# One address distance per stage, and 512-column matmuls in one up projection, in a two-layer hybrid decoder

## The chip, the cores and the metric

The kernel runs on one core of one Trainium2 chip. The metric is device time in microseconds (us) for one execution of the whole program; two runs of the kernel before gave 2269.54 and 2273.31 us, a median of 2271.43 us.

## The reference, cut to what matters

`x` has one sequence of 256 positions and 2048 channels, in float32. It goes through two layers and a last RMS norm. One layer is

```python
x = x + mixed(rms_norm(x) @ w_in) @ w_out            # w_in 2048 x 6400, w_out 2048 x 2048
h = rms_norm(x) @ w_up                               # 2048 x 11264
acc = conv_b + sum(conv_w[j] * shift(h, 2 - j) for j in range(3))
gate, val = split(acc, 2)
x = x + (silu(gate) * val) @ w_down                  # 5632 x 2048
```

`mixed` is three token mixers side by side (retention, dilated attention, a gated MLP over positions). They cost little here: the weights are 3168 blocks of 128 x 128 a layer, and nearly all of the time goes into multiplying each of them once with the 256 positions.

## The kernel before, in words

All activations are held transposed, channels on the 128 partitions and the 256 positions along the free axis (`S = 256`, `P = 128`). The program computes in float32 with TensorE's `float32r` type: every operand is split into a rounded high part and a low part, and a product is the sum of three matmuls, high times high, high times low and low times high.

**Weights.** They stream from HBM in 792 pieces of 128 x 1024 numbers, in the order of use (class `Weights`). ScalarE copies a piece to `hi` (line 113), VectorE subtracts to get `lo` (line 123). `hi` and `lo` have four buffers each, and a piece is split three pieces before its use. One piece is eight blocks of 128 x 128. `take` hands out the next block; at the first block of a piece it also calls `step`, and each call moves the evacuations that are under way on by one `yield`. So the order of instructions on ScalarE and VectorE is written out by this count and not by a scheduler.

**Projections with the activations moving** (`proj_t`, matmul at line 355). For a block of the weights the weights are loaded into the array, and 256 columns of the activation operand stream through. An operand tile holds its high part in the first 256 columns and its low part in the next 256. In layer 0 a block's three matmuls are `hi` with the high part, `hi` with the low part, `lo` with the high part; in layer 1 the order is `hi`, `lo`, `hi`. An output tile `m` takes 16 blocks (12 in the last part of the down projection), its sum stands in the first 256 of the 512 columns of a PSUM bank, and there are four such banks (`mm`). Operands are `p` tiles (the normalised input, for `w_in` and `w_up`) or `q` tiles (mixer outputs, for `w_out`; gated values, for `w_down`).

**Projections with the weights moving** (`proj_n`, matmul at line 395), for those parts of `w_in` whose result is wanted with positions on the partitions. Here the `p` tile is loaded and 256 columns of `hi` or `lo` stream.

**The FFN** runs in three parts of 16, 16 and 12 gated tiles (`FFN_PARTS`): up projection of a part, then its share of the down projection. `up_evac` takes an up projection's sum: `scaled` (line 366) multiplies it by the norm's factor `rbc` into `hs`, then come the convolution, the gate, and the split into a `q` tile (lines 736 and 738).

**The q tiles.** Sixteen slots in one pool; `q_tile` allots 2 * 256 + 112 float32 numbers, 2496 bytes in each partition, and returns 512 of them from a start that depends on `which`. There are eight values of `which`: `w_out`, and the three parts of `w_down`, in each of two layers.

Of the kernel before, what the change touches and what calls it, by code (L numbers as in the profile page):

```python
# [21 lines left out]
F32 = mybir.dt.float32  # L22
F32R = mybir.dt.float32r
AF = mybir.ActivationFunctionType
ALU = mybir.AluOpType
AX = mybir.AxisListType

P = 128
D = 2048
S = 256  # L30
# [123 lines left out]
def trunk_kernel(tc, x0, xt, stream, par, cst, wst, lnw, out):  # L154
# [3 lines left out]
    V, A, T, GP = nc.vector, nc.scalar, nc.tensor, nc.gpsimd  # L158
    ctx = ExitStack()
    with ctx:  # L160
        E = ctx.enter_context

        def pool(name, bufs=1):
            return E(tc.tile_pool(name=name, bufs=bufs))

        cp, xp, pp, qp = pool("cst"), pool("xres"), pool("px"), pool("qx")
# [25 lines left out]
        def until(cond):  # L192
            n = 0
            while not cond():
                n += 1
                assert n < 100
                step(0)
                step(1)

        def run(g):  # L200
            ev.append(g)

        W = Weights(nc, stream, raw, hp, lp, 3, step)
        live = [0]

        def mm():
            until(lambda: live[0] < 4)
            live[0] += 1
            return ps.tile([P, 512], F32, name="mm", tag="mm")

        def mt():
            return mm()[:, 0:S]
# [22 lines left out]
        make_identity(nc, ident)  # L235
        ones = cp.tile([P, P], F32, name="ones")
        GP.memset(ones, 1.0)
        mhalf = cp.tile([P, 12], F32, name="mhalf")
        GP.memset(mhalf, -0.5)
        hs_bufs = [cp.tile([P, S + 2], F32, name=f"hs{i}") for i in range(4)]  # L240
        for t in hs_bufs:
# [7 lines left out]
        norm = {"n": 0}  # L249
# [88 lines left out]
        def proj_t(mat, l, rows, cols, opnd, evac, lead):  # L338


            n = len(rows)
            groups = [list(range(lead))] + [[m] for m in range(lead, len(cols))]
            for g in groups:
                fast[0] = lead > 0 and W.pos > 0 and (len(g) > 1 or g[0] == len(cols) - 1)
                acc = {m: mt() for m in g}
                sz = 8 if len(g) > 1 else n
                for k0 in range(0, n, sz):
                    for m in g:
                        for k in range(k0, min(k0 + sz, n)):
                            x = opnd(k)  # L350
                            hi, lo = W.take(mat, l, rows[k], cols[m], P)
                            xh, xl = x[:, 0:S], x[:, S : 2 * S]
                            terms = ((hi, xh), (hi, xl), (lo, xh)) if l == 0 else ((hi, xh), (lo, xh), (hi, xl))
                            for i, (w, v) in enumerate(terms):
                                T.matmul(acc[m], w, v, start=k == 0 and i == 0, stop=k == n - 1 and i == 2)  # L355
                        if k == n - 1:
                            run(evac(m, acc[m]))

        def moved(acc):

            t = temp()
            A.activation(t, acc, AF.Copy)
            live[0] -= 1
            return t

        def scaled(acc, out):

            if norm["ready"]:
                V.tensor_tensor(out, acc, norm["bc"], op=ALU.mult)  # L369
                live[0] -= 1  # L370
            else:
                t = moved(acc)
                yield
                yield from normed()
                V.tensor_tensor(out, t, norm["bc"], op=ALU.mult)

        def normed():
            while not norm["ready"]:
                yield

        def temp():
            return fw.tile([P, S], F32, name="t", tag="t", bufs=4)
# [24 lines left out]
            return QX[k]  # L407


        STARTS = [b // 4 for b in (0, 128, 320, 384, 448, 64, 192, 256)]  # L410

        def q_tile(slot, which):
            a = STARTS[which]
            return qp.tile([P, 2 * S + 112], F32R, name=f"q{slot}", tag=f"q{slot}")[:, a : a + 2 * S]

        def mixed_block(slot, l, src, c0):

            t = mx()
            for j in range(2):
                T.transpose(t[:, j * P : (j + 1) * P], src[j][:, c0 : c0 + P], ident)  # L420
            q = q_tile(slot, 4 * l)
            w = prm[:, C_MIX + l * NK + slot : C_MIX + l * NK + slot + 1]
            yield
            split_hi(q, t[:, 0:S], w)
            split_lo(q, t[:, 0:S], w)
            QX[slot] = q
# [189 lines left out]
        for l in range(DEPTH):  # L616
# [8 lines left out]
            def att_qk(m, acc):  # L625
                h, half = m // 2, m % 2
                if half == 0:
                    aqk[h] = qp.tile([P, 2 * S], F32, name=f"aqk{h}", tag=f"q{Q_ATT + h}")
                yield from scaled(acc, aqk[h][:, half * S : (half + 1) * S])

            proj_t("w_in", l, allrows, [c + h * P for h in range(H) for c in (AQ, AK)], p_of, att_qk, 4)
            fast[0] = False

# [18 lines left out]
            def ret_qk(m, acc):  # L652
# [12 lines left out]
                V.tensor_tensor(o, o, sw, op=ALU.add)  # L665

            proj_t("w_in", l, allrows, [c + h * P for h in range(H) for c in (RQ, RK)], p_of, ret_qk, 0)

            rv = pair("rv", 768)
# [28 lines left out]

            PX[:] = [None] * NK
            proj_t("w_out", l, MIX_ROWS, [m * P for m in range(NK)], q_of, ev_out(C_N2 + l * NK), 4)  # L700

            norm["ready"] = False
# [9 lines left out]
            def up_evac(f0, part):  # L712
                gate = {}

                def ev_up(m, acc):
                    f, val = f0 + m // 2, m % 2
                    ch = f + NF * val
                    hs = hs_bufs[hsn[0] % len(hs_bufs)]
                    hsn[0] += 1
                    yield from scaled(acc, hs[:, 2 : S + 2])  # L720
                    yield
                    a = wk.tile([P, 512], F32, name="a", tag=A_TAGS[an[0] % 4])[:, 0:S]
                    an[0] += 1
                    A.activation(a, hs[:, 2 : S + 2], AF.Identity, scale=conv_col(ch, 2), bias=conv_col(ch, 3))  # L724
                    yield
                    V.scalar_tensor_tensor(a, hs[:, 1 : S + 1], conv_col(ch, 1), a, op0=ALU.mult, op1=ALU.add)  # L726
                    V.scalar_tensor_tensor(a, hs[:, 0:S], conv_col(ch, 0), a, op0=ALU.mult, op1=ALU.add)  # L727
                    yield
                    if val == 0:
                        A.activation(a, a, AF.Silu)  # L730
                        gate[f] = a
                        return
                    V.tensor_tensor(a, a, gate.pop(f), op=ALU.mult)  # L733
                    yield
                    q = q_tile(f - f0, part)
                    A.activation(q[:, 0:S], a, AF.Copy)  # L736
                    yield
                    V.tensor_tensor(q[:, S : 2 * S], a, q[:, 0:S].bitcast(F32), op=ALU.subtract)
                    QX[f - f0] = q
                return ev_up  # L740
# [15 lines left out]
        bc = norm["bc"][:, None, :].to_broadcast([P, 2, S])  # L756
# [93 lines left out]
```

## Time and profile before

| what | value |
| --- | --- |
| median of two runs | 2271.43 us |
| time of the profiled execution | 2269.97 us |
| its span, first to last instruction | 2268.2 us |
| TensorE busy, share of the span | 99% |
| matmuls | 19430 |
| VectorE busy, ScalarE busy | 64%, 50% |
| HBM read | 420.06 MB, 186 GB/s |
| granted TensorE clock, share of full speed | 0.998 |

A busy span of a matmul covers its whole way through the array, and the spans of successive matmuls overlap (a 256-column matmul is booked with 277 ns and the next begins some 113 to 120 ns later). So the busy share says that TensorE never waits long, but not how fast it works; the pace is read from the time that a counted run of matmuls took. The stages, by time in the trace: layer 0's `w_in` to 310 us, `w_out` to 402, then up and down projections by parts to 578 and 669, 843 and 934, 1065 and 1133 us. Layer 1: `w_in` to 1433, `w_out` to 1525, up and down to 1700 and 1791, 1965 and 2056, 2187 and 2255 us.

### The profile page before, as it was taken

To read this page: it belongs to the slowest core of one execution; us is meant where nothing else is said; L and a number is where in the kernel's file an instruction comes from. 1 tells how busy PE (TensorE), PEld (TensorE's weight loads), DVE (VectorE), ACT (ScalarE), POOL (GpSimd) and SP (SyncE) were. 2 spreads that over 40 slices of the span, in tenths; PEclk is the share of its full clock that TensorE was granted. 3 is DMA by queue.
4 is the path that set the end of the run, shared out by engine and by line. 5 is a ranking of instruction groups with operands and counts; after the bars stand their busy time and mean duration, and the time that the engine had idled before them with its cause. 6 is when DMAs were issued, how large, how long until landed. Compare 5 with 4: busy or idle time off the path is not lost.

```text
span 2268.2 us, 45995 instructions
## 1 busy us (share of the span) xinstructions
PE 2251.2 (99%) x19430; PEld 2248.1 (99%) x19430; DVE 1443.3 (64%) x2086; ACT 1143.5 (50%) x1616; POOL 21.8 (1%) x39
## 2 busy tenths in 40 slices
PE   9999999999999999999999999999999999999997
PEld 8999999999999999999999999999999999999997
DVE  6565556677547775577655655667775577656765
ACT  6475554555435553455544644555554355434553
POOL 0000000000000000000000001000000000000000
PEclk9999999999999999999999999999999999999999
DMA  8545445555555555565555454555555555555553
GB/s 283 193 158 187 160 168 194 188 194 195 186 186 196 195 182 197 179 206 189 184 201 180 164 180 168 178 184 192 193 192 188 185 199 193 194 186 189 193 191 126
DMA packets 117135, 425.15 MB, mean 187 GB/s; under 512 B 12992, under 2 KB 12992, under 8 KB 116800
## 3 DMA queue, kind: packets, MB, share of 16 engines
q1 hardware_dynamic: 116928, 422.21, 54.8%
q8 instruction: 152, 2.49, 0.4%
q14 instruction: 55, 0.45, 0.1%
HBM read 420.06 MB, written 2.10 MB: 186 GB/s over the span
## 4 chain that ended last, share of the span: by engine, by line
PE 99%; DMA 0%; DVE 0%; SPq 0%; ACT 0%; POOLq 0%; issue 0%; DVEq 0%
PE mm L355 84%; PE mm L395 13%; PE mx L420 0%; DMA xg<-in_xt_dram 0%; PE mx L435 0%; PE mx L489 0%; DVE xg L760 0%; PE mx L310 0%; PE mx L450 0%; PE mx L554 0%; PE mx L458 0%; PE mx L500 0%; PE mx L459 0%; PE mx L501 0%; PE mx L499 0%; PE mx L434 0%
## 5 line engine op out<-in xcount | busy, mean ns | idle before, releaser
L123 DVE TENSOR_TENSOR lo<-raw,hi 128x1024 fp32r<-128x1024 f32 (+1 forms) x793 | 969.0, 1223 | 710.4 <-ACT hi L113 710.2
L113 ACT ACTIVATE hi<-raw 128x1024 fp32r<-128x1024 f32 (+1 forms) x793 | 837.5, 1058 | 881.8 <-PE mm L355 490.7
L355 PE MATMUL mm<-p,hi 128*128 128x256 f32 x7168 | 1235.4, 277 | 5.5 <-ACT hi L113 5.2
L355 PEld LDWEIGHTS mm<-p,hi 128*128 128x128 f32 x7168 | 1084.6, 188 | 6.9 <-ACT hi L113 5.2
L355 PE MATMUL mm<-p,lo 128*128 128x256 f32 x3584 | 991.8, 277 | 0.0
L355 PE MATMUL mm<-q,hi 128*128 128x256 f32 x3840 | 684.8, 281 | 0.0
L355 PEld LDWEIGHTS mm<-p,lo 128*128 128x128 f32 x3584 | 674.3, 188 | 0.5 <-DVE lo L123 0.2
L355 PEld LDWEIGHTS mm<-q,hi 128*128 128x128 f32 x3840 | 589.3, 188 | 0.0
L355 PE MATMUL mm<-q,lo 128*128 128x256 f32 x1920 | 538.4, 280 | 0.0
L355 PEld LDWEIGHTS mm<-q,lo 128*128 128x128 f32 x1920 | 361.6, 188 | 0.0
L395 PE MATMUL mm<-hi,p 128*128 128x256 f32 x1664 | 272.1, 279 | 0.0
L395 PEld LDWEIGHTS mm<-hi,p 128*128 128x128 f32 x1664 | 231.2, 188 | 0.0
L395 PE MATMUL mm<-lo,p 128*128 128x256 f32 x832 | 179.3, 278 | 0.0
L724 ACT ACTIVATE a<-hs,prm 128x256 f32<-128x256 f32 x176 | 104.1, 591 | 63.3 <-DVE hs L369 63.3
L395 PEld LDWEIGHTS mm<-lo,p 128*128 128x128 f32 x832 | 133.3, 188 | 0.0
L727 DVE SCALAR_TENSOR_TENSOR a<-hs,prm,a 128x256 f32<-128x256 f32 x176 | 85.3, 485 | 6.3
L726 DVE SCALAR_TENSOR_TENSOR a<-hs,prm,a 128x256 f32<-128x256 f32 x176 | 84.2, 478 | 4.4 <-ACT a L724 4.4
L692 DVE TENSOR_TENSOR xg<-xg,mm 128x256 f32<-128x256 f32 x128 | 53.3, 418 | 50.7 <-PE mm L355 50.7
L369 DVE TENSOR_TENSOR hs<-mm,rbc 128x256 f32<-128x256 f32 x176 | 73.5, 418 | 2.7 <-PE mm L355 2.7
L730 ACT ACTIVATE a<-a 128x256 f32<-128x256 f32 x88 | 35.6, 405 | 33.5 <-DVE a L727 33.5
L279 ACT ACTIVATE t<-xg 128x256 f32<-128x256 f32 x75 | 30.1, 408 | 39.9 <-DVE xg L692 38.9
L736 ACT ACTIVATE q<-a 128x256 fp32r<-128x256 f32 x88 | 35.4, 403 | 3.5 <-DVE a L733 3.5
(120 smaller groups left out, 578.4 us busy)
## 6 DMA issues: line engine op xcount, KB each, us to landing
raw<-in_stream_dram SPq DMA_DIRECT2D x791, 512.0 KB, 3.4
out_dram<-xg SPq DMA_DIRECT2D x8, 256.0 KB, 2.4
xg<-in_xt_dram SPq DMA_DIRECT2D x3, 512.0 KB, 8.6
cs<-in_cst_dram SPq DMA_DIRECT2D x1, 1216.0 KB, 8.7
raw<-in_stream_dram SPq DMA_DIRECT2D x2, 256.0 KB, 4.2
ws<-in_wst_dram SPq DMA_DIRECT2D x2, 256.0 KB, 4.5
lw<-in_lnw_dram SPq DMA_DIRECT2D x2, 256.0 KB, 4.7
prm<-in_par_dram SPq DMA_DIRECT2D x1, 412.0 KB, 6.0
```

The costliest lines, as they stand in the source:

```text
L113: self.nc.scalar.activation(hi[:, h], src[:, h], AF.Copy)
L123: self.nc.vector.tensor_tensor(lo[:, h], src[:, h], hi[:, h].bitcast(F32), op=ALU.subtract)
L279: A.activation(sq, X[j], AF.Square)
L355: T.matmul(acc[m], w, v, start=k == 0 and i == 0, stop=k == n - 1 and i == 2)
L369: V.tensor_tensor(out, acc, norm["bc"], op=ALU.mult)
L395: T.matmul(acc[j][:, c], v, w[:, c], start=k == 0 and i == 0 and c.start == 0, stop=k == NK - 1 and i == 2, skip_group_check=True)
L692: V.tensor_tensor(X[m], X[m], acc, op=ALU.add)
L724: A.activation(a, hs[:, 2 : S + 2], AF.Identity, scale=conv_col(ch, 2), bias=conv_col(ch, 3))
L726: V.scalar_tensor_tensor(a, hs[:, 1 : S + 1], conv_col(ch, 1), a, op0=ALU.mult, op1=ALU.add)
L727: V.scalar_tensor_tensor(a, hs[:, 0:S], conv_col(ch, 0), a, op0=ALU.mult, op1=ALU.add)
L730: A.activation(a, a, AF.Silu)
L736: A.activation(q[:, 0:S], a, AF.Copy)
```

## The change

It has three parts.

1. A `q` slot is 2 * 256 + 128 numbers, 2560 bytes, five times 512. All slots then start at the same address modulo 512, and so do all the operands of one `which`. `STARTS` is written as the wanted distance `r` less 192.
2. In the up projection of layer 1 (`wide`), a block's two matmuls with `hi` become one with 512 columns, high and low part of the operand side by side; its sum fills all 512 columns of the bank. The matmul with `lo` adds to the first 256. For the last block of an output tile the `lo` matmul comes first. `scaled` then copies the second half of the bank to a temporary on ScalarE, and VectorE adds the first half to it before the multiplication with `rbc`.
3. `mhalf` is 2 columns wide, where it was 12.

```diff
-        mhalf = cp.tile([P, 12], F32, name="mhalf")
+        mhalf = cp.tile([P, 2], F32, name="mhalf")
...
-                acc = {m: mt() for m in g}
+                wide = mat == "w_up" and l == 1
+                acc = {m: mm() if wide else mt() for m in g}
...
                             hi, lo = W.take(mat, l, rows[k], cols[m], P)
+                            if wide:
+                                if k == n - 1:
+                                    T.matmul(acc[m][:, 0:S], lo, x[:, 0:S], start=False, stop=False)
+                                T.matmul(acc[m], hi, x, start=k == 0, stop=k == n - 1)
+                                if k < n - 1:
+                                    T.matmul(acc[m][:, 0:S], lo, x[:, 0:S], start=False, stop=False)
+                                continue
...
         def scaled(acc, out):
 
-            if norm["ready"]:
+            if acc.shape[1] > S:
+                t = temp()
+                A.activation(t, acc[:, S : 2 * S], AF.Copy)
+                yield
+                V.tensor_tensor(t, t, acc[:, 0:S], op=ALU.add)
+                live[0] -= 1
+                yield from normed()
+                V.tensor_tensor(out, t, norm["bc"], op=ALU.mult)
+            elif norm["ready"]:
                 V.tensor_tensor(out, acc, norm["bc"], op=ALU.mult)
...
-        STARTS = [b // 4 for b in (0, 128, 320, 384, 448, 64, 192, 256)]
+        STARTS = [(r - 192) % 512 // 4 for r in (448, 128, 256, 0, 160, 64, 384, 224)]
 
         def q_tile(slot, which):
             a = STARTS[which]
-            return qp.tile([P, 2 * S + 112], F32R, name=f"q{slot}", tag=f"q{slot}")[:, a : a + 2 * S]
+            return qp.tile([P, 2 * S + 128], F32R, name=f"q{slot}", tag=f"q{slot}")[:, a : a + 2 * S]
```

The places of the tiles in the built programs, as bytes modulo 512 within a partition. "Distance" is the operand's start less the weights' start, modulo 512, which all blocks of a stage share where the last column names one value, since pieces, blocks and the two halves of an operand are multiples of 512 bytes.

| tile or stage | before | after |
| --- | --- | --- |
| `hi`, `lo` blocks | 0 | 480 |
| `p` tiles | 192 | 160 |
| distance `p` to weights (`w_in`, `w_up`) | 192 | 192 |
| `q` slots in the order of memory | 192, 128, 64, 0, 448, ... (64 less each) | 160, all |
| distance in `w_out`, layer 0 | all eight multiples of 64 | 448 |
| in `w_down`, layer 0, three parts | all eight multiples of 64 | 128; 256; 0 |
| in `w_out`, layer 1 | all eight multiples of 64 | 160 |
| in `w_down`, layer 1, three parts | all eight multiples of 64 | 64; 384; 224 |

Before, a stage's operands come in an order in which the distance mostly falls by 64 from one block to the next. In the first part of layer 0's `w_down` it is 320, 256, 192, 128, 64, 0, 64, 0 for slots 0 to 7; in the last part of layer 1's it is 448 for slot 0, then 384.

TensorE's order at the start of layer 1's up projection (`p` and `q` are operand tiles, `hi` and `lo` weights, `mm` the sums), before:

```order
L355 MATMUL mm<-q_17577,hi_18432 128x256
L355 MATMUL mm<-p_17643,hi_18466 128x256
L355 MATMUL mm<-p_17643,lo_18467 128x256
L355 MATMUL mm<-p_17643,hi_18466 128x256
L355 MATMUL mm<-p_17679,hi_18466 128x256
L355 MATMUL mm<-p_17679,lo_18467 128x256
L355 MATMUL mm<-p_17679,hi_18466 128x256
```

The same place in the changed program:

```order
L363 MATMUL mm<-q_17577,hi_18432 128x256
L356 MATMUL mm<-p_17643,hi_18466 128x512
L358 MATMUL mm<-p_17643,lo_18467 128x256
L356 MATMUL mm<-p_17679,hi_18466 128x512
L358 MATMUL mm<-p_17679,lo_18467 128x256
```

Three matmuls of 256 columns for a block became one of 512 and one of 256, with one weight load less; there are 1408 blocks in this projection, and nothing else changed its place on TensorE.

VectorE's order over the first two evacuations of the same projection (`t` is the temporary, `a` the convolution's sum, `lo` the split of a later piece), before:

```order
L123 TENSOR_TENSOR lo_18713<-raw_18580,hi_18712 128x1024
L369 TENSOR_TENSOR hs_124<-mm,rbc 128x256
L123 TENSOR_TENSOR lo_18746<-raw_18610,hi_18745 128x1024
L726 SCALAR_TENSOR_TENSOR a<-hs_124,prm,a 128x256
L727 SCALAR_TENSOR_TENSOR a<-hs_124,prm,a 128x256
L369 TENSOR_TENSOR hs_125<-mm,rbc 128x256
```

The same place in the changed program:

```order
L123 TENSOR_TENSOR lo_18681<-raw_18580,hi_18680 128x1024
L380 TENSOR_TENSOR t<-t,mm 128x256
L383 TENSOR_TENSOR hs_124<-t,rbc 128x256
L123 TENSOR_TENSOR lo_18707<-raw_18602,hi_18706 128x1024
L742 SCALAR_TENSOR_TENSOR a<-hs_124,prm,a 128x256
L743 SCALAR_TENSOR_TENSOR a<-hs_124,prm,a 128x256
L380 TENSOR_TENSOR t<-t,mm 128x256
L383 TENSOR_TENSOR hs_125<-t,rbc 128x256
```

Each evacuation has one VectorE instruction more, the addition, and stands one `step` later in the program, behind a copy `t<-mm` on ScalarE (line 378 of the changed kernel).

## Rows read from the trace of the kernel before

**Rows 1.** The page, busy time by engine.

```profile
PE 2251.2 (99%) x19430; PEld 2248.1 (99%) x19430; DVE 1443.3 (64%) x2086; ACT 1143.5 (50%) x1616; POOL 21.8 (1%) x39
```

**Rows 2.** Chain of waits, layer 1's up projection: start us, us, engine, tile, line, count.

```profile
1534.27 165.94 PE mm L355 x1464
...
1790.89 174.32 PE mm L355 x1538
...
2055.78 130.92 PE mm L355 x1155
```

**Rows 3.** Chain of waits in the eight stages on q tiles, in their order.

```profile
319.62 82.64 PE mm L355 x696
...
577.58 91.41 PE mm L355 x769
...
843.00 91.02 PE mm L355 x769
...
1064.48 67.55 PE mm L355 x568
...
1442.28 82.28 PE mm L355 x695
...
1700.10 90.91 PE mm L355 x768
...
1964.98 91.03 PE mm L355 x769
...
2186.47 68.64 PE mm L355 x578
```

**Rows 4.** Chain of waits within layer 0's input projection and mixers.

```profile
130.82 2.74 PE mm L355 x24
...
134.89 2.83 PE mm L355 x24
...
187.32 32.64 PE mm L395 x288
...
229.58 14.14 PE mm L395 x120
```

**Rows 5.** The same chain, matmuls on plain float32 operands.

```profile
120.29 0.33 PE mx L450 x3
...
134.45 0.43 PE mx L435 x2
```

**Rows 6.** Timeline of TensorE, first part of layer 0's down projection: start us, length.

```profile
580.14 0.41 PE L355 MATMUL mm<-q,hi 128*128 128x256 f32 x2
580.38 0.29 PE L355 MATMUL mm<-q,lo 128*128 128x256 f32 x1
580.51 0.40 PE L355 MATMUL mm<-q,hi 128*128 128x256 f32 x2
```

**Rows 7.** Timeline of TensorE, entry into layer 1's last down projection.

```profile
2186.42 0.28 PE L355 MATMUL mm<-p,hi 128*128 128x256 f32 x1
2186.53 0.28 PE L355 MATMUL mm<-q,hi 128*128 128x256 f32 x1
2186.65 0.28 PE L355 MATMUL mm<-q,lo 128*128 128x256 f32 x1
2186.76 0.40 PE L355 MATMUL mm<-q,hi 128*128 128x256 f32 x2
```

**Rows 8.** Busy time by engine in an up projection of layer 1, clock, DMA.

```profile
1790.90:1965.10 174.20, 174.20 (x1539) 174.20 (x1539) 125.15 (x187) 91.95 (x126) 0.00 (x0) 1.00 0.58 192
```

**Rows 9.** Groups by line: busy us, mean ns of one, idle before.

```profile
L362 ACT ACTIVATE t<-mm 128x256 f32<-128x256 f32 x28 | 10.8, 385 | 44.4 <-PE mm L355 40.8 <-PE mx L310 3.3 <-DVE sqacc L284 0.2
...
L733 DVE TENSOR_TENSOR a<-a 128x256 f32<-128x256 f32 x88 | 36.8, 418 | 0.2
```

**Rows 10.** Timeline of VectorE, last operand of layer 1's last part.

```profile
2192.21 0.42 DVE L738 TENSOR_TENSOR q<-a,q 128x256 fp32r<-128x256 f32 x1
```

## The prediction

> **What bounds the kernel now.** First the page: TensorE and its weight loads are busy for 99% of the span, VectorE for 64%, ScalarE for 50% [rows 1]. So no stage waits long for weights or evacuations, and the time is the number of matmuls times the interval between their starts. The chain of waits gives that interval, since it counts matmuls in unbroken stretches. In layer 1's up projection it is 165.94 / 1464 = 113.3 ns, and the same in the other two parts [rows 2]. In the eight stages whose moving operand is a `q` tile, it is 118.7, 118.9, 118.4, 118.9, 118.4, 118.4, 118.4 and 118.8 ns [rows 3], with the same instruction, the same 256 columns and the same weight buffers. The clock is granted in full, at its 2.4 GHz level [rows 8], where 256 columns are 106.7 ns; so 6.6 ns are lost with a `p` operand and some 12 with a `q` operand.
>
> What differs is the address. `p` operands keep one distance to the weights, `q` operands change it from block to block. But distance is not all. With one and the same distance, TensorE has two intervals: weights that stream against `p` tiles take 32.64 / 288 = 113.3 ns at 187 us and 14.14 / 120 = 117.8 ns at 230 us, after float32 matmuls of the retention came between; and runs of 24 with `p` moving take 2.74 or 2.83 us, 117.9 ns at the longer, after interruptions alike [rows 4]. I read this as a rhythm of the two read streams, weights and moving operand, that either settles (113.3) or does not (117.8), and that stays as it is until something interrupts it. A step in distance interrupts it at each block: one block's three matmuls after such a step took 0.37 us, from 580.14 to 580.51 [rows 6], or 123 ns each. But a step from 192 to 448 did not: at the entry into the last part the starts go on at 0.11, 0.12 and 0.11 us [rows 7].
>
> **The change, term by term.** The sum is made against the profiled execution, 2269.97 us, which is 1.5 us under the median of 2271.43; I give the result against the median.
>
> *The wide up projection.* Each of 1408 blocks now takes three intervals, 0.340 us [rows 2]. It will take one matmul of 512 columns and one of 256. No row has 512 columns of this type. Nearest is the plain float32 matmul of 256 columns, which takes about twice as long as a `float32r` one: two take 0.43 us, so 0.215 to 0.22 each [rows 5], with one weight load beside each. With a settled 113.3 for the short one this makes 0.330 us, with an unsettled 117.8 it makes 0.335. I take the middle, 0.3325, since the new pair has two unequal windows and neither rhythm is shown for it: 7.5 ns less, 1408 x 7.5 ns = 10.6 us. Upper bound: the short one at the pace of 128-column float32 matmuls, 0.33 / 3 = 0.110 [rows 5], together 0.325, a gain of 21 us. Lower bound: the short one at the worst 0.123 [rows 6] and the long one at 0.220, 0.343, a loss of 4 us.
>
> A rule speaks against the size of this gain. The Trainium skill, "TensorE: Matmul & The Clock Gate", Back-to-back issue gap, gives a warm matmul N / 2.4 + 2.5 ns; then a merge saves one 2.5 ns, an estimate of 1408 x 2.5 = 3.5 us. It would also put 256 columns at 109 ns, and the trace, with 113.3 and 118.4, does not agree.
>
> *The evacuation of the wide sums.* It adds 88 copies on ScalarE, 385 ns each, and 88 additions on VectorE at 418 ns [rows 9]: 34 and 37 us. They lie beside the matmuls. In the part at 1791 us VectorE is busy for 125.15 of 174.20 us and ScalarE for 91.95 [rows 8]; 32 evacuations add 13.4 and 12.3 us, and in a stage of some 170 us that is 81% and 61%. The copy waits for the sum in ScalarE's queue ahead of the split of a piece that is used three pieces, over 8 us, later. The chain to the next operand grows by one step, at most a piece of 24 matmuls or 2.7 us [rows 4]. The latest operand of the last part is finished at 2192.63 us [rows 10], and slot 11 is first read 105 matmuls after the stage's start at 2186.53 [rows 7], at 118.8 ns each 2199.0; so 6.4 us of cover become 3.7. Cost zero. If the cover were gone, each of the three parts would wait for the excess, one to three us in all. A sum's bank is held up to one piece longer; with four banks and 5.3 us an output tile, that delays nothing.
>
> *The q stages.* 5760 matmuls take 683 us at the intervals of rows 3. What one distance makes of each, no row shows except for 192 and, at the entry, 448. Bounds: the settled 113.3 for all, 653 us, a gain of 30.5 us; the worst block's 123 for all, 708 us, a loss of 25 us. I take by stage:
> - 448, `w_out` of layer 0: settled, by [rows 7]; 768 x 5.4 ns = 4.1 us.
> - 160 and 224, in layer 1: 32 bytes from 192, nearer to it than any other stage, but no operand of the kernel before has such a distance. I take half of the way to 113.3: 768 x 2.55 + 576 x 2.75 ns = 3.5 us.
> - 128, 256, 0, 64 and 384: unsettled, 117.8, since all that [rows 4] has for an interruption of unknown phase is the one or the other, and the q stages pass through these distances without settling. 768 x (1.1 + 0.6 + 0.6 + 0.6) + 576 x 1.1 ns = 2.9 us.
>
> Together 10.5 us. The row 123 is far from these, since it follows a step up in distance, and steps are what goes.
>
> The Trainium skill, "SBUF — State Buffer", Who interferes with whom, says that "PE and ACT never wait on anyone" and gives TensorE independent read ports for weights and moving operand. By that, distance changes nothing and this term is 0. The two intervals of like instructions in rows 2 and 3 speak against it, though they do not prove the address to be the cause.
>
> `STARTS`, `mhalf` and the longer slots add no instruction; DMAs keep their number, size and order. The weights' buffers start 32 bytes off their former place, for a DMA share of 0.58 [rows 8], which has cover.
>
> Sum: 10.6 + 10.5 = 21 us; 2271.4 - 21 = **2250 us** (2249 for a profiled execution like that before).
>
> **The rivals.**
> - *All eight stages settle.* For: 113.3 holds for whole up projections; nothing interrupts a stage of `w_down`. Against: the unsettled 14.14 us stretch also had one distance. 30.5 us, and 13.4 with a settled pair of 0.3305: 2227.5 us.
> - *The distance does nothing*, as the page's rule has it, or the rhythm of no stage settles: the q stages keep their time. For: both intervals occur at equal distance [rows 4]. Against: [rows 2, 3]. 2271.4 - 10.6 = 2261 us.
> - *The merged matmul pays little*: the loss is a part of each 256 columns, and the long matmul loses it twice; 2.5 ns remain a block, 3.5 us. For: [rows 5] is of another type, which takes twice the time for as many columns. Then 2271.4 - 3.5 - 10.5 = 2257 us.
> - *Slower: the shift by 32 bytes spoils the up projection.* `p` and weights keep 192 between them, but both now start 32 bytes past a multiple of 64, and no row has such operands. If reads go by longer lines, each stream touches one more. The 7680 matmuls of 256 columns that run at 113.3 now (4224 in layer 0's `w_up`, 2304 with `p` and 1152 with weights moving in `w_in`) would go to 117.8 and cost 34.6 us; with a wide pair of 0.335 (7 us) and q stages at 117.8 (4.6 us) that is 2294 us. It decides from 21 us / 7680 = 2.7 ns on, an interval of 116.0 in the up projection of layer 0. Against: the distance itself is the same.
>
> **How the numbers follow.** The forecast has 0.46, all settled 0.15, no effect of distance 0.19, little from the merge 0.12, slower 0.06, and 0.02 for what I did not think of. The likeliest is 2250 us. The range reaches down to 2228, where all settle, and up to 2266, where the distance does nothing and the merge half of its due; outside are half of the all-settled cases, the slower rival and the odd ones, not quite 0.2. The mark of 2%, about what a measurement of this kernel can tell from no change, lies at 2226 and 2317 us. Faster than that needs all settled and a pair of under 0.330: 0.06. Slower than that needs over 120 ns in the up projection of layer 0: 0.02.
>
> **What would show it.** Layer 1's up projection: blocks of 0.33 us, near 468 us of matmuls where there were 479, VectorE near 81%, no wait at its ends. `w_out` of layer 0: 113.3 ns but for the stretch with interruptions; distances 160 and 224 between 113 and 118; the other five near 117.8. Layer 0's up projection still at 113.3. The forecast is wrong if a stage with one distance goes above 119, if the pair stays at 0.34, or if matmuls of layer 0's up projection take over 114 ns.

## The result, and the profile after

The changed kernel takes 2298.05 us (median of two runs, 2297.86 and 2298.23), where the kernel before takes 2271.43 us. The ratio is 1.0117, with a 95% interval of 1.0074 to 1.0161: 26.6 us slower, outside the forecast range of 2228 to 2266 us. The granted clock is 0.998 in both. The first line of the page shows that TensorE is still the bound, now with fewer and partly longer matmuls; it answers to [rows 1].

```profile
PE 2279.6 (99%) x18022; PEld 2210.8 (96%) x18022; DVE 1474.5 (64%) x2174; ACT 1176.2 (51%) x1704; POOL 21.8 (1%) x39
```

So the time must be in the intervals between matmuls. The table takes each stage of the two traces from its first matmul to the first of the next stage, with the mean interval between starts of 256-column matmuls. "Distance" is the operand's start less the weights', modulo 512.

| stage | before, us (ns) | after, us (ns) | difference, us |
| --- | --- | --- | --- |
| `w_in`, layer 0, all | 304.92 | 307.65 | +2.7 |
| of it, first run of 576 on `p` | 71.89 (113.65) | 73.62 (116.79) | +1.7 |
| `w_out`, layer 0, distance 448 | 91.96 (118.77) | 87.92 (113.47) | -4.0 |
| up, layer 0, part 1 | 175.54 (113.42) | 182.02 (117.64) | +6.5 |
| up, layer 0, parts 2 and 3 | 304.68 (113.35) | 304.67 (113.35) | 0.0 |
| down, layer 0: 128; 256; 0 | 91.31; 90.91; 68.52 | 91.14 (118.67); 92.14 (119.98); 69.10 (119.97) | +1.6 |
| `w_in`, layer 1, all | 299.77 | 303.00 | +3.2 |
| `w_out`, layer 1, distance 160 | 91.69 (118.40) | 91.86 (118.64) | +0.2 |
| up, layer 1, the wide one | 175.53; 174.09; 130.56 | 181.96; 180.68; 135.51 | +18.0 |
| down, layer 1: 64; 384; 224 | 90.91; 90.93; 68.27 | 90.45 (117.77); 91.14 (118.67); 68.04 (118.33) | -0.5 |
| sum | | | +27.7 |

The spans differ by 28.0 us (2268.2 and 2296.2), so the table holds nearly all of it. Three things made it: the wide up projection lost 18.0 us, three stages that the change did not seem to touch lost 12.4, and the q stages gained 2.7 where 10.5 were forecast.

**The wide matmul.** TensorE's timeline of the changed kernel, first blocks of layer 1's up projection after an interruption by the norm (start us, length, operation). The length covers the way through the array; what counts is the time from start to start.

```profile
1541.45 0.39 PE L356 MATMUL mm<-p,hi 128*128 128x512 f32 x1
1541.67 0.28 PE L358 MATMUL mm<-p,lo 128*128 128x256 f32 x1
1541.79 0.39 PE L356 MATMUL mm<-p,hi 128*128 128x512 f32 x1
1542.02 0.28 PE L358 MATMUL mm<-p,lo 128*128 128x256 f32 x1
1542.14 0.39 PE L356 MATMUL mm<-p,hi 128*128 128x512 f32 x1
1542.37 0.28 PE L358 MATMUL mm<-p,lo 128*128 128x256 f32 x1
1542.48 0.40 PE L356 MATMUL mm<-p,hi 128*128 128x512 f32 x1
1542.72 0.28 PE L358 MATMUL mm<-p,lo 128*128 128x256 f32 x1
1542.84 0.40 PE L356 MATMUL mm<-p,hi 128*128 128x512 f32 x1
```

The first pair takes 0.34 us, as three settled matmuls did in [rows 2]; the fourth takes 0.36. Over the whole projection the long one takes 234.4 ns and the short one 118.5: 0.3529 us a block where it was 0.3400. 1408 blocks by 12.9 ns are 18 us. Twice the settled 113.3 is 226.7 and twice the unsettled 117.8 is 235.6: the merged matmul costs about what two of the slow kind cost, and the short one beside it is slow too.

**The q stages.** The chain of waits, within each of the eight stages in their order (start us, us, engine, tile, line, count), answers to [rows 3]. Divided, they give 113.4, 118.7, 120.0, 120.0, 118.7, 117.8, 118.7 and 118.3 ns.

```profile
321.89 77.20 PE mm L363 x681
...
584.00 89.12 PE mm L363 x751
...
848.98 90.12 PE mm L363 x751
...
1071.94 67.08 PE mm L363 x559
...
1453.91 80.10 PE mm L363 x675
...
1716.92 89.16 PE mm L363 x757
...
1988.90 89.12 PE mm L363 x751
...
2214.95 67.09 PE mm L363 x567
```

**The stages nobody touched.** In `w_in` and in layer 0's up projection order, tiles and distance to the weights are as before. The chain of the changed kernel through the first of each, from the norm's interruption on (`mx`, float32 matmuls on `ones`):

```profile
35.99 0.43 PE mx L320 x2
36.42 42.17 PE mm L363 x358
...
406.23 0.79 PE mx L310 x8
407.01 2.93 PE mm L363 x24
409.95 0.43 PE mx L320 x2
410.38 171.72 PE mm L363 x1458
```

And of the kernel before, at the same places:

```profile
36.02 0.43 PE mx L320 x2
36.45 40.59 PE mm L355 x358
...
411.43 0.43 PE mx L320 x2
411.87 165.15 PE mm L355 x1457
```

With the same interruption ahead, the changed kernel comes out at 42.17 / 358 = 117.8 and 171.72 / 1458 = 117.8 ns, the one before at 113.4 and 113.3, and each stays there to the end of the stage.

**The evacuation** cost nothing, as forecast. The same part as in [rows 8], by windows (busy us of PE, its loads, DVE, ACT, POOL; clock, DMA share, GB/s):

```profile
1807.00:1987.60 180.60, 180.60 (x1026) 157.11 (x1025) 136.15 (x218) 104.35 (x157) 0.00 (x0) 1.00 0.54 187
```

TensorE has no gap. VectorE went from 125.15 to 136.15 us, 75% of the stretch, ScalarE from 91.95 to 104.35. The last operand of the last part answers to [rows 10]:

```profile
2221.77 0.42 DVE L754 TENSOR_TENSOR q<-a,q 128x256 fp32r<-128x256 f32 x1
```

It is there at 2222.19; by the count used in the prediction it is first read at 2214.31 + 105 x 0.1183 = 2226.7 us. Of 6.4 us of cover 4.5 are left.

### The profile page after: what moved, and what is told of

Its sections match the earlier page's. It is cut to its first block, busy times and chain, and to the rows that moved or that the text cites. A ratio compares the mean times of both kernels' runs of the same rounds, so it can differ in the third digit from the quotient of the medians.

```text
span 2296.2 us, 43356 instructions
## 1 busy us (share of the span) xinstructions
PE 2279.6 (99%) x18022; PEld 2210.8 (96%) x18022; DVE 1474.5 (64%) x2174; ACT 1176.2 (51%) x1704; POOL 21.8 (1%) x39
## 4 chain that ended last, share of the span: by engine, by line
PE 98%; DVE 0%; ACT 0%; DMA 0%; issue 0%; SPq 0%; POOLq 0%; DVEq 0%
PE mm L363 62%; PE mm L356 14%; PE mm L411 13%; PE mm L358 7%; PE mm L355 0%; PE mx L436 0%; DMA xg<-in_xt_dram 0%; PE mx L451 0%; PE mx L505 0%; ACT p L257 0%; DVE xg L776 0%; PE mx L310 0%; PE mx L466 0%; PE mx L570 0%; PE mx L320 0%
## 5 line engine op out<-in xcount | busy, mean ns | idle before, releaser
L363 PE MATMUL mm<-p,hi 128*128 128x256 f32 x4352 | 764.9, 280 | 5.2 <-ACT hi L113 5.1
L363 PEld LDWEIGHTS mm<-p,hi 128*128 128x128 f32 x4352 | 664.9, 189 | 6.8 <-ACT hi L113 5.0
L363 PE MATMUL mm<-p,lo 128*128 128x256 f32 x2176 | 606.9, 279 | 0.1
L356 PE MATMUL mm<-p,hi 128*128 128x512 f32 x1408 | 491.2, 397 | 0.0
L363 PEld LDWEIGHTS mm<-p,lo 128*128 128x128 f32 x2176 | 409.9, 188 | 1.0 <-DVE lo L123 0.7
L358 PE MATMUL mm<-p,lo 128*128 128x256 f32 x1320 | 371.2, 281 | 0.0
L356 PEld LDWEIGHTS mm<-p,hi 128*128 128x128 f32 x1408 | 258.6, 188 | 56.6
L358 PEld LDWEIGHTS mm<-p,lo 128*128 128x128 f32 x1320 | 247.8, 188 | 3.8
```

The lines of the kernel that those rows point to most:

```text
L356: T.matmul(acc[m], hi, x, start=k == 0, stop=k == n - 1)
L358: T.matmul(acc[m][:, 0:S], lo, x[:, 0:S], start=False, stop=False)
```

## The experiments

Four questions: which parts of the change cost what; whether the distance decides, or something else that goes with it; why a shift by 32 bytes costs anything; and whether a 512-column matmul can pay at all. Where no interval stands, the time is that of one execution; the kernel before then took 2270.2 to 2272.9 us beside it.

### The change without the wide matmul

```diff
-                wide = mat == "w_up" and l == 1
+                wide = False
```

> The changed kernel with its up projection of layer 1 in 256-column matmuls again; the one distance per stage and the narrower mhalf stay. Theory (the pair of 512 and 256 columns is itself slower, 0.3528 us a block where three matmuls took 0.3400): 18 us come back, 2298 - 18 = 2280 us, and layer 1's up projection is at 113.3 ns. Rival (the new place of the tiles slows that projection whatever the columns): it stays at 117.5 to 118.5 ns, and the time at 2295 to 2298 us.

Measured 2279.68 us, ratio to before 1.0038 [1.0023, 1.0053]. Layer 1's up projection is back at 113.5, 113.3 and 113.4 ns; every other stage is as in the changed kernel. So the starts and `mhalf` alone make it slower by 8.7 us.

### The wide matmul alone, in the kernel before

```diff
+                wide = mat == "w_up" and l == 1
...
-        STARTS = [(r - 192) % 512 // 4 for r in (448, 128, 256, 0, 160, 64, 384, 224)]
+        STARTS = [b // 4 for b in (0, 128, 320, 384, 448, 64, 192, 256)]
```

(the changed kernel's matmuls and evacuation; starts, slots and `mhalf` of before)

> The kernel before with the 512-column matmuls alone; q slots of 2496 bytes and mhalf as before. Theory (the pair itself is slower): 2271 + 18 = 2289 us, 235 and 118 ns for the pair. Rival (the pair loses only after the shift of all tiles by 32 bytes): 0.330 to 0.335 us a block, 2257 to 2264 us.

Measured 2288.58 us, ratio 1.0079 [1.0062, 1.0096]: 17.6 us. The pairs are those of the changed kernel (234.4 and 118.5 ns), and the other stages are those of before. With the 8.7 us above that is 26.3 of the 26.6 us: the two parts add up.

### `mhalf` alone

```diff
-        mhalf = cp.tile([P, 12], F32, name="mhalf")
+        mhalf = cp.tile([P, 2], F32, name="mhalf")
```

> The kernel before with mhalf two columns wide, so that all later tiles start 32 bytes lower and all distances stay. Theory (only distances and the order of events count): every stage as before, 2271 us within 2. Rival (the start modulo 64 counts): layer 0's first part of the up projection at 117.6 ns in place of 113.4 (6.5 us) and the first stretches of both input projections near 117 ns (6 us), 2283 us.

Measured 2288.0 us. The theory fell: a tile of constants, made smaller by 40 bytes, costs 17 us. Its chain through layer 0's first up part reads

```profile
413.35 171.72 PE mm L355 x1458
```

which is 117.8 ns, the same as in the changed kernel. Layer 1's `w_in` (117.4 and 117.8 ns in its first two runs) and its first up part (182.02 us) are slow as well; the q stages and the other up parts are as before. The rival came nearer, but not stage by stage: it had layer 0's `w_in` slow, which settled here behind the norm, and not layer 1's first up part, which was struck. And operands off a multiple of 64, the mechanism of the prediction's slower rival, would have struck all up parts alike.

What did change is this: `ones`, `ident` and the parameters are placed ahead of `mhalf` and stay, while everything placed behind it (the norm's sums, `p`, `q`, weights) moves by 32 bytes. In the norm's float32 matmuls `ones` had the distance 320 to the sums, and now 352.

### Everything moved by 32 bytes

```diff
+        pad = cp.tile([P, 8], F32, name="pad")
         prm = cp.tile([P, NPAR], F32, name="prm")
```

> The kernel before with an unused tile of 32 bytes ahead of all others, so that every tile moves by 32 bytes, the constants ones and ident with the rest. With mhalf alone narrowed (c_shift32), ones and ident stayed where they were, and the first parts of the up projection went to 117.6 ns after the norm's matmuls on ones. Theory (the distance between the interrupting matmuls' own tiles and the weights decides in which rhythm TensorE leaves an interruption): all distances are as before, so 2271 us and 113.4 ns there. Rival (the start modulo 64 of operands counts): 2283 to 2290 us.

Measured 2269.76 us, and every stage has its interval of before to within 0.1 ns; layer 0's first up part is

```profile
411.66 164.35 PE mm L356 x1450
```

113.3 ns. Where tiles start modulo 64 does not matter, so my slower rival's mechanism is refuted. What stands between tiles does.

### The changed kernel with `ones` and `ident` moved along

```diff
-        warm = cp.tile([P, 2], F32, name="warm")
         shim = gap.tile([P, 32], F32, name="shim")
         GP.memset(shim, 0.0)
+        warm = shim[:, 0:2]
...
-        mhalf = cp.tile([P, 2], F32, name="mhalf")
+        mhalf = cp.tile([P, 12], F32, name="mhalf")
```

> The changed kernel, but `mhalf` has its 12 columns again and `warm` lies inside `shim`: operands, weights and buffers keep the changed kernel's places, while `cs`, `ident`, `ones` move 32 bytes back, so that every float32 matmul of the norm and the mixers has the distances of the kernel before. Theory: it is those distances by which TensorE comes out of an interruption settled or not. Then layer 0's `w_in` (113.6, 113.3) and first up part (113.4 ns) settle again: 2298 less 12.4 us (6.5 + 2.7 + 3.2) is 2286 us, with the wide pair and the q stages unchanged. Rival: operands 32 bytes past a multiple of 64 leave an interruption unsettled by themselves: it stays at 2298 us, with 117.4 to 117.8 ns in these stages.

Measured 2285.73 us, 0.3 from the theory's number. Operands and weights lie as in the changed kernel, but the stages are settled again:

```profile
36.90 40.14 PE mm L363 x354
...
408.07 165.03 PE mm L363 x1456
```

113.4 and 113.3 ns. So the 12.4 us come back with the places of the interrupting float32 matmuls' tiles. Two things are restored together here, the distance within those matmuls (320) and theirs to `p` and the weights; which of them counts stays open.

Nor do the places alone fix the state. The kernel with `mhalf` alone and the change without the wide matmul have the same narrow `mhalf`, and come out of the same interruptions differently. First the former, then the latter, each in layer 0's `w_in` and in layer 1's first up part:

```profile
37.84 40.82 PE mm L355 x360
...
1545.90 171.13 PE mm L355 x1453
...
35.97 42.41 PE mm L363 x360
...
1543.98 165.03 PE mm L363 x1456
```

That is 113.4 and 117.8 ns in the one, 117.8 and 113.3 ns in the other. What else decides is not shown.

### All q operands at distance 192

```diff
-            a = STARTS[which]
-            return qp.tile([P, 2 * S + 112], F32R, ...)[:, a : a + 2 * S]
+            a = 0
+            return qp.tile([P, 2 * S], F32R, ...)[:, a : a + 2 * S]
```

> The kernel before with q slots of 2048 bytes and no starts, so that all q operands have the distance 192 of the p operands. Theory (a constant distance of 192 lets a stage settle at 113.3 ns): all eight stages at 113.3, 2271 - 30 = 2241 us; up to 2252 if an interruption leaves two or three stages at 117.8. Rival (the q stages are slow for another reason than the distance): 2271 us, 118.5 ns.

Measured 2240.72 us, ratio 0.987 [0.9855, 0.9884]: 30.3 us faster than before, the best of all kernels here. First and last down part:

```profile
575.99 85.11 PE mm L355 x751
...
2161.94 63.13 PE mm L355 x557
```

113.3 ns each; so have all eight q stages, with 113.6 as the mean over either `w_out`. One address is enough, and it needs less memory than either kernel.

### Other distances for q

```diff
-        STARTS = [(r - 192) % 512 // 4 for r in (448, 128, 256, 0, 160, 64, 384, 224)]
+        STARTS = [(r - 192) % 512 // 4 for r in (200, 96, 176, 184, 32, 196, 208, 188)]
```

(without the wide matmul)

> The changed kernel without 512-column matmuls, q operands at the distances 200, 96, 176, 184, 32, 196, 208, 188. Theory (settling needs a distance near 192 modulo 256, and 160 and 224 were outside of the window): 184 to 200 at 113.3 ns, 176 and 208 possibly, 32 and 96 at 118 to 120; 2255 to 2265 us. Rival (only exactly 192 modulo 256 settles): all eight at 117.5 to 120, 2282 us.

Measured 2306.49 us. In this order 120.0, 120.0, 119.3, 120.0, 116.7, 120.0, 119.2 and 118.5 ns: none settles. The two nearest to 192, at 196 and 188:

```profile
1728.98 90.12 PE mm L363 x751
...
2223.89 66.13 PE mm L363 x558
```

Four bytes off cost 120.0 and 118.5 ns. "Near 192" means nothing. The time is 24 us above even the rival's: three up parts that are settled in the change without the wide matmul run at 117.7 to 117.8 ns here, which is 20 us, two of them behind stages at 96 and 196. What one stage leaves behind may carry into the next; no run tests that by itself.

### The same distance for all, by moving the weights

```diff
-        shim = gap.tile([P, 32], F32, name="shim")
+        shim = gap.tile([P, 40], F32, name="shim")
```

in the kernel with all q at 192: distance 160 in every projection, `p` and `q` in their places.

> The kernel with all q operands at distance 192, but `shim` is 32 bytes longer, so that the weights lie 32 bytes further on and every projection, with p and with q operands, has distance 160. Theory: the distance of the moving operand to the weights decides, whatever the operand. Then p stages too run at 118.6 ns, where they had 113.3: 9600 p matmuls and 5760 q matmuls by 5.2 ns are 80 us, 2321 us in all (2315 to 2335, the stages with weights moving being unknown). Rival: what matters is the p and q tiles' own place, which stays as it was: 2241 us.

Measured 2354.98 us. A down part and an up part:

```profile
599.96 90.12 PE mm L355 x751
...
692.00 183.12 PE mm L355 x1526
```

120.0 ns in both: the direction is the theory's, the size is not, which took 118.6 from the one stage at 160 in the changed kernel. Distance decides whatever the operand is: 32 bytes between constants and weights cost 114 us against the kernel at 192. With 256 bytes more instead, distance 448:

```diff
-        shim = gap.tile([P, 32], F32, name="shim")
+        shim = gap.tile([P, 96], F32, name="shim")
```

> The same with `shim` 256 bytes longer: distance 448 everywhere. Theory: 448 is 192 modulo 256 and settles like it: 2241 us (2236 to 2250, since interruptions may leave a stage at 117.8 ns), up and down projections at 113.3. Rival: only 192 itself is good, and the one q stage at 448 that settled did so by its entry: 2270 us or more.

Measured 2243.66 us, and the same two stages

```profile
578.89 85.11 PE mm L355 x751
...
664.91 173.17 PE mm L355 x1528
```

run at 113.3 ns. Most of the 2.9 us over the kernel at 192 is lost in layer 0's `w_in` (117.7 to 117.8 ns in its first two runs). Whether the distance or chance put it there is open: four executions of the kernel at 192 lie between 2240.33 and 2243.93 us. So 448 equals 192, and the stages of the changed kernel agree with a period of 256: 128 and 384 both 118.67, 256 and 0 both 119.97 to 119.98 ns.

### All q at 64

```diff
-        STARTS = [(r - 192) % 512 // 4 for r in (448, 128, 256, 0, 160, 64, 384, 224)]
+        STARTS = [(r - 192) % 512 // 4 for r in (64, 64, 64, 64, 320, 320, 320, 320)]
```

in the kernel with `ones` and `ident` moved along, without the wide matmul.

> The kernel i_near_moved without the wide matmul, with the q operands of layer 0 at distance 64 and those of layer 1 at 320, which is 64 modulo 256. Theory: of the distances only 192 modulo 256 can settle; the q stages run at 117.8 ns, as the one stage at 64 did: 5760 x 4.45 ns over the kernel with all at 192, 2266 us. Rival: 64 is the same pair of places with the roles exchanged (weights moving at distance 320 run at 113.34 ns in one stretch of `w_in`), and settles where nothing interrupts: 2241 us, q stages at 113.3; or in the down projections only after an entry that favours it, 2241 to 2266.

Measured 2268.68 us; all eight q stages run at 117.78 ns, here one of each layer:

```profile
580.99 89.04 PE mm L363 x756
...
1964.98 89.04 PE mm L363 x756
```

The theory's number holds to 3 us. The q operands run at the unsettled interval of [rows 4], and none of the eight stages settles, at 64 or at 320.

### The wide matmul at eight distances

```diff
-                wide = mat == "w_up" and l == 1
+                wide = mat in ("w_out", "w_down")
...
-        STARTS = [(r - 192) % 512 // 4 for r in (448, 128, 256, 0, 160, 64, 384, 224)]
+        STARTS = [(r - 192) % 512 // 4 for r in (192, 128, 0, 64, 160, 224, 32, 96)]
```

VectorE adds both halves of a sum to the residual.

> The changed kernel with the 512-column matmul in w_out and w_down in place of the up projection, at the distances 192, 128, 0, 64, 160, 224, 32, 96 (eight stages in their order); the residual takes two additions. Theory (the long matmul loses per column, so that a pair can at best take three intervals of 113.3): no distance gives a block under 0.340 us, 192 gives 0.353; 2251 to 2275 us. Rival (192 is a bad distance for a pair, another suits it): some stage at 0.325 to 0.333 us a block; with all at that 2232 us.

Measured 2287.63 us. Pairs of 352.8, 351.3, 351.8, 352.5, 347.3, 352.1, 347.9 and 350.6 ns; the long matmul takes 229.8 to 234.8. None is under the 0.340 us of three settled matmuls. The time is above the theory's range, since layer 0's first up part and layer 1's first two also run at 117.6 to 117.8 ns. At distances other than 192 the pair is shorter than three matmuls are (347.3 against three at 118.6 or 120.0 at 160), so merging is worth something only where the separate ones are slow.

### Half the weight load

```diff
+                                if mat == "w_up" and l == 1 and i == 1:
+                                    T.matmul(acc[m][0:64], w[:, 0:64], v, start=False, stop=False)
+                                    continue
```

in the kernel at 192. It leaves the `lo` correction out for half of the output channels of layer 1's up projection.

> The kernel with all q operands at distance 192 (d_all192, 2240.7 us), where the lo matmul of layer 1's up projection loads 64 weight columns and not 128, and so leaves out that correction for half of the output rows. Theory (the weight load's reads collide with the moving operand's): the matmul beside which only 64 columns are loaded takes less than 113.3 ns, 108 to 111, and the stage gains 3 to 7 us if the other two stay settled. Rival (the loss of 6.6 ns belongs to streaming 256 columns and not to the load): all three at 113.3, 2241 us.

Measured 2267.98 us. The page's groups of loads in it, of 128 and of 64 columns (line, operation, count, busy, mean ns):

```profile
L358 PEld LDWEIGHTS mm<-p,hi 128*128 128x128 f32 x7168 | 1090.6, 188 | 6.9 <-ACT hi L113 5.1
...
L356 PEld LDWEIGHTS mm<-p,lo 128*64 128x64 f32 x1408 | 194.2, 138 | 0.0
```

A load of half the columns is 50 ns shorter and gives nothing back: in the 16 settled blocks ahead of the norm's interruption the intervals stay 113.3 ns, and in the unsettled ones behind it 117.8. On this the rival holds; the 6.6 ns over 106.7 are not the length of the load. Unasked it showed something else. After the norm's interruption in layer 1's first up part TensorE came out unsettled and stayed so for the rest of the program, over 730 us, through down projections whose instructions and distances are those of the kernel at 192:

```profile
1687.99 89.04 PE mm L358 x756
...
2184.89 67.13 PE mm L358 x570
```

117.8 ns where that kernel has 113.3; this makes the 27 us over the rival's 2241 us.

## Why the prediction was wrong

**The wide pair: the failed step.** I priced a 512-column `float32r` matmul from plain float32 ones [rows 5], another type, and took 0.3325 us for a block, with 0.343 as the worst. It is 0.3529, as the wide matmul alone shows: +18.0 us in place of -10.6, a miss of 28.6 of the 48 us between forecast and result. Rows of the same type were there: two unsettled matmuls [rows 4] are 0.2356, and with an unsettled short one the pair has 0.353 for an upper bound. I had assumed that a pair at distance 192 would be settled, or half so. The rival on the merge ("loses it twice") had the right idea, but for it, too, I let the short matmul keep its settled pace. The row was also misread: line 435 issues one float32 matmul of 256 columns for each of six heads in two layers, 12 in all, and the trace counts 24. So the 0.215 us are half of such a matmul and not a whole one, which takes about four times as long as a `float32r` one and not twice.

By the Trainium skill, "TensorE: Matmul & The Clock Gate", Back-to-back issue gap, 512 columns in isolation take N / 2.4 + 2.5, an estimate of 215.8 ns; here they take 229.8 to 234.8 at eight distances, and the measurement decides.

**The edit counted at nothing: `mhalf`.** I wrote that it adds no instruction, and weighed the shift of the weights for its DMA share alone. It cost 12.4 us, by [rows 4]'s own reading: the state after an interruption is one or the other, and the addresses of the tiles in the interruption have a part in it. The kernel with `ones` moved along returns the 12.4 us. They are not all of it: `mhalf` alone, in the kernel before, cost 17 us and struck other stages. My slower rival named the shift and one of its stages, and its 2294 us came near the result by accident: it had +34.6 for the shift, -7 for the wide pair and -4.6 for the q stages, where the runs have +12.4, +18.0 and -2.7. Its mechanism fell with the shift of all tiles together.

**The q stages: 10.5 us forecast, 2.7 measured.**
- 448 was right: 4.0 us, 4.1 forecast. The trace of before had more for it than the one entry of [rows 7]: in that stage of layer 1 slot 0, at 448, comes back behind slower blocks and takes 0.340 us again (at 2189.38 and 2192.22 us), where the seven blocks between take 0.353 to 0.362. So a step in distance need not unsettle, and can settle.
- 160 and 224 "half of the way" was wrong: 118.64 and 118.33 ns, worth 0.1 us in place of 3.5. Closeness in bytes has no meaning; 188 and 196 do not settle either.
- The other five at 117.8 was right for 64 (117.77); 128 and 384 are 118.67, and 256 and 0 are 119.97 to 119.98, worse than the mixture of before. Together they cost 1.4 us, with 2.9 forecast as a gain. That a single distance can be worse than a mixture was in my bounds (123), but not in my choice. The reason given against it was misread: by the list of distances, the block at 580.14 us [rows 6] is slot 7, at distance 0 behind 64, which is a step down and not up.

All three signs that I had named for a wrong forecast came: stages above 119 ns, a pair no better than 0.34 us, and layer 0's first up part at 117.6 ns.

**What held.** TensorE bound throughout; the reading of the trace as a rhythm that settles or not and then stays (the half-load kernel shows it staying for 730 us at one distance); that 448 equals 192; the upper bound of 30.5 us for all eight settled, measured 30.3 with one start for all; the evacuation at no cost, with 4.5 us of cover where 3.7 were forecast.

**No effect of the distance** was given 0.19. The kernels at 160 and at 192 differ in the place of the weights alone and by 114 us. The Trainium skill, "SBUF — State Buffer", Who interferes with whom, has it that "PE and ACT never wait on anyone", in a passage on engines that wait for each other; for TensorE's own two reads, of weights and moving operand, the traces show that the address counts: 113.3 against 120.0 ns for like instructions.

## What to carry to other kernels

- Divide the chain's unbroken stretches of matmuls by their counts. If like matmuls have two or three intervals, look at the distance between moving operand and weights modulo 256; here 192 gave 113.3 ns, or 117.8 where it did not settle, and all others 116.7 to 120.0 over a whole stage. Then give every operand that one distance.
- A tile of constants that changes its size moves whatever is placed behind it against whatever is placed ahead. To cost such an edit at nothing, one needs the addresses of all tiles that TensorE reads, those of rare matmuls too.
- Price a new shape by rows of its own type, in the worst state these rows show, before borrowing from another type.

## What the runs showed of the hardware that was not expected

With full clock (0.998), 256 columns of `float32r` and a weight load for each, the interval has fixed levels: 113.33, 117.78 and 120.0 ns, which at 2.4 GHz are 272, 282.7 and 288 periods. Some distances lie between (116.7, 118.5, 118.67, 119.2). The distance between operand and weights acts with a period of 256 bytes and to the last 4 of them. At 192 two states are stable, 113.33 and 117.78, taken at an interruption and kept until the next one or until a stage at another distance; at 64 only 117.78 was seen with q moving, though weights moving against `p` at 320 run 113.34 in some stretches of `w_in`. Some 11 us into the traces the same instructions start only every 213.3 ns, in the kernel at 160 as in that at 192, so the distance does not show there; the clock reads 1.00 there too, and no row tells why the pace is half. At 160 one stage had 118.64 among others at 192, and the whole program 120.0, so a distance does not fix the value alone. Why 192 is the good one, what the 6.6 ns over 106.7 are that even the settled state loses, and why the 512-column matmul leaves its first pace of two settled ones, none of these runs tells.
